# A depthwise convolution stage with tokens in eight phases and block-Toeplitz weights, on eight Trainium2 cores

## The chip, the cores and the metric

The kernel runs on all 8 cores of one Trainium2 chip. Each core takes half of one of the four sequences, that is 2048 tokens plus a halo, and no core talks to another. The metric is device time in microseconds (us) of the slowest core. A program on all eight cores has a second, slower state in some executions: the cores of one die, or of both, show a lower granted TensorE clock, and the time is some per cent longer. A ratio is the mean time of one kernel's fast runs over the mean of the other's of the same rounds, so it is not quite the ratio of the medians quoted beside it. The brackets behind a ratio are its 95% interval.

## The reference, cut to what matters

The function is one encoder block. Only the convolution branch and the pooling branch matter here; the gates, the output projections and the SwiGLU part are unchanged in what they compute.

```python
def conformer_conv(a_val, a_gate, w_dw, b_dw, ln_g, ln_b, w_conv_out):
    a = a_val * jax.nn.sigmoid(a_gate)                       # (B, T, 1024)
    pad = CONV_KERNEL // 2                                   # CONV_KERNEL = 31
    a = lax.conv_general_dilated(
        a, w_dw[:, None, :].astype(a.dtype), window_strides=(1,), padding=[(pad, pad)],
        dimension_numbers=("NWC", "WIO", "NWC"), feature_group_count=a.shape[-1]) + b_dw
    a = jax.nn.silu(layer_norm(a, ln_g, ln_b))               # over the channels
    return a @ w_conv_out

# multi_scale_pool: for four channel groups, a centred window mean (windows 2, 4, 8, 16)
# over the tokens minus the token itself, then linear maps.      [...]
```

## The kernel before

Activations lie with 128 channels on the partitions and tokens along the free axis. The 1024 channels are 8 blocks of 128. One block of the convolution stage is: project value and gate (80 matmuls of 416 columns, in five pieces), multiply value by sigmoid(gate) into `aT`, store that to `ad` in device memory, and load it back four times, shifted by 0 to 3 tokens, as an im2col operand `rep` with 32 channels by 4 shifts on the partitions. The convolution of the block before runs between two projections. It multiplies `rep` with weights that GpSimd builds from a mask. Four matmuls of 32 output channels run side by side in four column tiles of the PE array.

```python
def vg(c):                                   # value and gate of block c
    for p in range(NPC):                     # 5 pieces of 416 tokens
        ...                                  # 8 + 8 matmuls into two PSUM banks
        act(s_, bg_[:, 0:PW], AF.Sigmoid)
        tt(DVE, aT[c % 2][:, sl], bv[:, 0:PW], s_, ALU.mult)
        if p == 2:
            a_out(c, 0, 3 * PW)              # SyncE stores the first three pieces
        pump(2)                              # two queued pooling-window operations on VectorE
    a_out(c, 3 * PW, EXT)

def conv(c):
    pump_until(win_done, c)
    for b in range(NB):                      # 4 tiles of 512 tokens
        ps = nb()
        for q in range(8):
            for j in range(4):               # 4 column tiles of 32 channels
                ...                          # matmul 128x32 weights, 512 columns
        act(d_sb[c][b][:], ps[:], AF.Identity, bias=pcc(PC_BDW, c))
        ...                                  # squares; sums on VectorE for the LayerNorm
        pump(1)
    if c + 2 < KC:
        build_cw(c + 2)                      # GpSimd multiplies mask and weights

for c in range(1, KC):
    vg(c)
    conv(c - 1)
    im2col(c)                                # SyncE: wait for the stores, 8 loads
```

Three dots mark cuts, here and in the other listings. DMA work is issued in order by the engine named in the call: SyncE (`SP`) for activations, GpSimd (`POOL`) for weights.

## Time and profile before

| | before |
|---|---|
| time, median of 3 | 1033.84 us (1032.79 to 1034.22) |
| span of the profiled core (core 7) | 1039.7 us |
| TensorE busy | 1005.6 us, 97% |
| one block of the convolution stage | 21.2 us = 14.17 + 7.02 |

The profile's page of the kernel before: busy time, then the span in 40 slices with the busy share in tenths (and for PEclk the granted clock in tenths), then DMA packets, then the chain of work that ended last by engine and by line.

```profile
span 1039.7 us, 15674 instructions; the slowest of 8 cores (1026.0 to 1039.7 us)
...
PE 1005.6 (97%) x5696; PEld 489.7 (47%) x5696; DVE 450.1 (43%) x693; ACT 307.6 (30%) x500; POOL 158.0 (15%) x182
...
PE   3899999999999999999999999999999999999997
...
PEclk9999999999989999999999999999999999999999
...
DMA packets 34251, 99.90 MB, mean 96 GB/s; under 512 B 3968, under 2 KB 7168, under 8 KB 31616
...
PE 91%; DMA 4%; DVE 2%; ACT 1%; issue 1%; SPq 0%; POOL 0%; DVEq 0%; ACTq 0%; POOLq 0%
PE ps L353 86%; PE ps L628 5%; DMA rep_186<-ad 2%; DMA xb_178<-xp 1%; DVE uT L374 1%; DMA ad<-aT_183 1%; DVE sqx L367 1%; DMA wslot_68<-w_pool_out 0%; ACT sqx L364 0%; ACT ps L364 0%; DVE h2b_259 L374 0%; ACT L364 0%; SPq L190 0%; ACT zt_197 L364 0%; ACT zt_203 L364 0%
```

The chain is TensorE almost alone: between the first two slices and the last there is none below 9 tenths. The chain in order of time (start, duration, what) shows the block's period. L353 is the projection, L628 the convolution.

```profile
142.44 7.02 PE ps L628 x128
149.46 14.17 PE ps L353 x80
163.63 7.02 PE ps L628 x128
170.66 14.17 PE ps L353 x80
```

The busy time by stretch (columns: stretch, length, then busy us and instructions of PE, PEld, DVE, ACT, POOL, then clock, DMA share and GB/s) shows that VectorE is nearly as full as TensorE in this stage.

```profile
156.00:182.00 26.00, 26.00 (x237) 13.73 (x236) 24.85 (x37) 8.70 (x15) 6.48 (x3) 1.00 0.67 144
182.00:208.00 26.00, 26.00 (x265) 13.52 (x266) 25.03 (x36) 8.20 (x15) 7.62 (x5) 1.00 0.69 149
```

So in the middle of the convolution stage, from about 144 to 222 us, three resources are near their limits at once: TensorE at 100%, VectorE at 24.85 and 25.03 of 26 us, and the DMA engines at two thirds. (Before and after that VectorE has 11 to 19 busy us in 26.) TensorE's gaps over 0.4 us from 92 to 309 us add up to 4.1 us.

### The profile page before, as it was taken

To read this page: it belongs to the slowest core of one execution; us is meant where nothing else is said; L and a number is where in the kernel's file an instruction comes from. 1 tells how busy PE (TensorE), PEld (TensorE's weight loads), DVE (VectorE), ACT (ScalarE), POOL (GpSimd) and SP (SyncE) were. 2 spreads that over 40 slices of the span, in tenths; PEclk is the share of its full clock that TensorE was granted. 3 is DMA by queue.
4 is the path that set the end of the run, shared out by engine and by line. 5 is a ranking of instruction groups with operands and counts; after the bars stand their busy time and mean duration, and the time that the engine had idled before them with its cause. 6 is when DMAs were issued, how large, how long until landed. Compare 5 with 4: busy or idle time off the path is not lost.

```text
span 1039.7 us, 15674 instructions; the slowest of 8 cores (1026.0 to 1039.7 us)
## 1 busy us (share of the span) xinstructions
PE 1005.6 (97%) x5696; PEld 489.7 (47%) x5696; DVE 450.1 (43%) x693; ACT 307.6 (30%) x500; POOL 158.0 (15%) x182
## 2 busy tenths in 40 slices
PE   3899999999999999999999999999999999999997
PEld 1645555555434444444444444444444444444486
DVE  4542789974278532233546521212121221342454
ACT  2643333343487612211144311111111111121121
POOL 2143122221420000000167001111000000000000
PEclk9999999999989999999999999999999999999999
DMA  9705876667254111111887446655222202403112
GB/s 215 212 1 94 177 165 145 149 155 157 50 88 65 31 31 31 31 21 21 209 317 154 100 79 96 95 85 83 35 35 34 32 1 92 151 39 124 81 82 82
DMA packets 34251, 99.90 MB, mean 96 GB/s; under 512 B 3968, under 2 KB 7168, under 8 KB 31616
## 3 DMA queue, kind: packets, MB, share of 16 engines
q0 software_dynamic: 17888, 45.10, 24.6%
q1 hardware_dynamic: 16288, 53.81, 17.8%
q8 instruction: 47, 0.77, 0.3%
q14 instruction: 28, 0.23, 0.1%
HBM read 111.93 MB, written 21.04 MB: 128 GB/s over the span
## 4 chain that ended last, share of the span: by engine, by line
PE 91%; DMA 4%; DVE 2%; ACT 1%; issue 1%; SPq 0%; POOL 0%; DVEq 0%; ACTq 0%; POOLq 0%
PE ps L353 86%; PE ps L628 5%; DMA rep_186<-ad 2%; DMA xb_178<-xp 1%; DVE uT L374 1%; DMA ad<-aT_183 1%; DVE sqx L367 1%; DMA wslot_68<-w_pool_out 0%; ACT sqx L364 0%; ACT ps L364 0%; DVE h2b_259 L374 0%; ACT L364 0%; SPq L190 0%; ACT zt_197 L364 0%; ACT zt_203 L364 0%
## 5 line engine op out<-in xcount | busy, mean ns | idle before, releaser
L353 PE MATMUL ps<-mT,weff 128*128 128x512 bf16 x256 | 60.7, 386 | 0.0
L353 PE MATMUL ps<-uT,wslot_60 128*128 128x512 bf16 (+6 forms) x224 | 51.8, 356 | 5.9 <-DVE uT L374 5.3
L353 PE MATMUL ps<-uT,wslot_65 128*128 128x512 bf16 (+6 forms) x216 | 47.1, 366 | 0.0
L364 ACT ACTIVATE sgf_225<-ps 128x512 f32<-128x512 f32 x30 | 17.9, 597 | 81.3 <-PE ps L353 77.6
L364 ACT ACTIVATE sgf_226<-ps 128x512 f32<-128x512 f32 x29 | 17.3, 597 | 82.1 <-PE ps L353 82.1
L364 ACT ACTIVATE sgf_227<-ps 128x512 f32<-128x512 f32 x29 | 17.3, 597 | 79.8 <-PE ps L353 79.8
L353 PE MATMUL ps<-uT,wslot_61 128*128 128x416 bf16 (+6 forms) x192 | 40.6, 358 | 0.0
L353 PEld LDWEIGHTS ps<-mT,weff 128*128 128x128 bf16 x256 | 25.4, 99 | 31.4 <-issue 4.6
L353 PE MATMUL ps<-uT,wslot_62 128*128 128x416 bf16 (+6 forms) x192 | 39.5, 352 | 0.0
L353 PE MATMUL ps<-uT,wslot_64 128*128 128x416 bf16 (+6 forms) x192 | 38.8, 346 | 0.0
L353 PE MATMUL ps<-vT,wslot_64 128*128 128x512 bf16 x160 | 38.2, 382 | 0.0
L353 PE MATMUL ps<-vT,wslot_62 128*128 128x512 bf16 x160 | 38.2, 382 | 0.0
L353 PE MATMUL ps<-vT,wslot_67 128*128 128x512 bf16 x160 | 38.1, 380 | 0.0
L353 PE MATMUL ps<-vT,wslot_66 128*128 128x512 bf16 x160 | 38.0, 380 | 0.0
L353 PEld LDWEIGHTS ps<-uT,wslot_60 128*128 128x128 bf16 x224 | 21.8, 98 | 34.2 <-issue 16.1
L353 PE MATMUL ps<-vT,wslot_63 128*128 128x512 bf16 x160 | 37.8, 379 | 0.0
L353 PE MATMUL ps<-vT,wslot_68 128*128 128x512 bf16 x160 | 37.8, 379 | 0.0
L353 PE MATMUL ps<-vT,wslot_65 128*128 128x512 bf16 x160 | 37.8, 379 | 0.0
L353 PE MATMUL ps<-vT,wslot_61 128*128 128x512 bf16 x160 | 37.8, 379 | 0.0
L353 PEld LDWEIGHTS ps<-uT,wslot_65 128*128 128x128 bf16 x216 | 21.3, 100 | 22.5 <-issue 3.2
L353 PE MATMUL ps<-uT,wslot_68 128*128 128x416 bf16 (+1 forms) x144 | 30.9, 357 | 0.0
L353 PE MATMUL ps<-vT,wslot_60 128*128 128x512 bf16 x128 | 30.2, 379 | 0.0
(1681 smaller groups left out, 1973.7 us busy)
## 6 DMA issues: line engine op xcount, KB each, us to landing
rep_185<-ad SPq DMA_DIRECT2D x32, 263.0 KB, 6.2
rep_186<-ad SPq DMA_DIRECT2D x32, 263.0 KB, 7.5
h2b_259<-h1d SPq DMA_DIRECT2D x2, 2048.0 KB, 9.1
h1b_216<-xr POOLq DMA_DIRECT2D x1, 2048.0 KB, 14.1
h1b_217<-xr SPq DMA_DIRECT2D x1, 2048.0 KB, 15.6
h1b_218<-xr SPq DMA_DIRECT2D x1, 2048.0 KB, 19.2
h1b_219<-xr SPq DMA_DIRECT2D x1, 2048.0 KB, 24.3
h1d<-h1b_216 SPq DMA_DIRECT2D x1, 2048.0 KB, 15.3
```

Of the source, the lines that this page charges most:

```text
L353: S.op(PE, lambda e: e.matmul(out, lhsT=lhsT, rhs=rhs, start=start, stop=stop), [lhsT, rhs], [out], signal=stop if signal is None else signal)
L364: S.op(ACT, lambda e: e.activation(out=out, in_=in_, func=func, scale=scale, **kw), reads, [out])
L367: S.op(eng, lambda e: e.tensor_tensor(out=out, in0=a, in1=b, op=op), [a, b], [out])
L374: S.op(eng, lambda e: e.scalar_tensor_tensor(out=out, in0=a, scalar=s, in1=b, op0=op0, op1=op1), [a, b] + ([] if isinstance(s, float) else ...
L628: S.op(PE, lambda e, o=o, lt=lt, r_=r_, q=q, j=j: e.matmul(o, lhsT=lt, rhs=r_, start=(q == 0), stop=(q == 7), tile_position=(0, 32 * j)), ...
```

## The change

The intent is to do the convolution with fewer, fuller matmuls. Tokens are kept in phase order throughout: token 8n + h goes to phase h, column n. In the convolution the 128 partitions then hold 16 channels by 8 phases. The 31 taps of one channel become a banded (Toeplitz) matrix from 8 input phases to 8 output phases, for five column shifts. A group of 16 channels is five 128x128 matmuls of 256 columns, and a block is 8 groups, so 40 matmuls instead of 128. The price is:

- The layout on the partitions changes twice. `a` goes to device memory piece by piece and comes back permuted as `aP`; the results go out as `dst` and come back permuted as `dall`. All of this is issued by SyncE, in order. A block's results are four tiles of two groups each, and there are three buffers `dst`. So ScalarE can evict the fourth tile (copy it out of PSUM, where the matmuls write) only when the store of the first tile, called store 0 below, has landed.
- The Toeplitz weights `cw` come from device memory, 2.6 MB of float32 a block, cast to 1.3 MB of bfloat16 by the DMA that GpSimd issues.
- The pooling windows cannot run over one row of tokens any more; each step splits in two at the phase boundary.

The core of the diff, with cuts marked:

```diff
-    aT = [at(f"aT{i}", [128, EXT], BF16, z + i * EXT * 2) for i in range(2)]
-    rep = [...]
+    cw = [at(f"cw{i}", [128, NG, NSH, 128], BF16, o) for i, o in enumerate((oW + 4096, oZ))]
+    aT = [at(f"aT{i}", [128, PW], BF16, z + i * PW * 2) for i in range(NAT)]      # NAT = 6
+    aP = [at(f"aP{i}", [128, NG, PN], BF16, z + i * NG * PN * 2) for i in range(2)]
+    dst = [at(f"dst{i}", [128, 2, ON], F32, z + i * 2048) for i in range(3)]      # three buffers
 [...]
+    def load_cw(c):
+        S.dma(POOL, cw_sem[c % 2], cw[c % 2][:].rearrange("p g s m -> p (g s m)"), cw_d.ap()[c])
 [... in vg(c), per piece p:]
-            tt(DVE, aT[c % 2][:, sl], bv[:, 0:PW], s_, ALU.mult)
-            pump(2)
+            tt(DVE, aT[r][:], bv[:, 0:PW], s_, ALU.mult)
+            S.dma(SP, ad_sem[r], a_d.ap()[c].rearrange("g (q h) n -> (g q) (h n)", h=NPH)[:, sl], aT[r][:])
+            pump(4)
 [... at its end:]
+        for p in range(NPC):
+            S.wait_prod(SP, ad_sem[(NPC * c + p) % NAT])
+        S.dma(SP, rep_sem[c % 2], aP[c % 2][:], a_d.ap()[c].rearrange("g p n -> p g n"))
 [... conv(c):]
+        for t in range(4):
+            ps = nb()
+            for i in range(2):
+                for s_ in range(NSH):
+                    mm(ps[:, i * ON:(i + 1) * ON], cw[c % 2][:, 2 * t + i, s_, :],
+                       aP[c % 2][:, 2 * t + i, s_:s_ + ON], s_ == 0, s_ == NSH - 1, ...)
+            r = (4 * c + t) % 3
+            [... ScalarE evicts the tile to dst[r] and its squares to dsq; VectorE adds both to sums]
+            S.dma(SP, dw_sem[r], dc_d.ap()[c][2 * t:2 * t + 2].rearrange("g p n -> p g n"), dst[r][:])
             pump(1)
+        for r in range(3):
+            S.wait_prod(SP, dw_sem[r])
+        S.dma(SP, dr_sem[c], dall[c][:], dc_d.ap()[c].rearrange("g (q h) n -> (g q) (h n)", h=NPH))
         if c + 2 < KC:
-            build_cw(c + 2)
+            load_cw(c + 2)
```

## The prediction

> **What bounds it now.** TensorE is busy 97% of the span and makes 91% of the chain that ended last, at a granted clock of 0.99. The change touches the convolution stage, about 92 to 290 us. By the timeline, one channel block there lasts 21.2 us: 80 value/gate matmuls of 416 columns (14.17 us) and 128 convolution matmuls of 128x32 weights (7.02 us; four column tiles run together). VectorE is just as full: 24.9 and 25.0 of 26 us busy from 156 to 208 us (busy time by stretch). TensorE hardly waits in this stage: 0.6 us before convolution 0 and 1.7 us before the last one, both for the im2col loads. DMA is busy 67 to 78%.
>
> **What the change removes.** A block's convolution becomes 40 matmuls of 256 columns. The output projection's 256-column bf16 matmuls start 0.109 us apart in this trace, so 4.36 us in place of 7.02: 2.66 us a block, 21 us in all. The four-fold im2col loads (2.1 MB a block, 145 ns a 2104-byte packet) go, and so does GpSimd's weight building, beside which one VectorE add took 2.1 us in place of 0.87.
>
> **What it adds**, a block:
> - DMA: ready Toeplitz weights, 1.3 MB after the cast (128 packets; the 5632-byte cast packets took 436 ns, so about 6.3 us of all 16 engines); convolution results out in 1024-byte packets (46 ns: 2.9 us) and back (8192-byte, 309 ns: 2.5 us); a permuted load in 520-byte packets (estimate 2 us); `a` out, 1.5 us; projection weights as before, 2.8 us. The sum, an estimate, is 18 us in a period that ought to be 18.6.
> - VectorE: the pooling windows go from 84 adds and subtractions to 164 smaller ones. Dependent ones start n/0.96 ns + 0.26 us apart, so I estimate 89 us in place of 81. With 4 issued a piece, a block needs 19 to 22 us. VectorE, not TensorE, then sets the pace, which alone cancels most of the gain.
> - A new wait. SyncE issues in order: last `a` piece, wait for it to land, permuted load, then the four result stores. The stores use three buffers, so ScalarE's eviction of tile 3 waits until store 0 lands, and holds a PSUM bank, the sigmoids and VectorE's sums behind it. Unloaded: 2.3 (an `a` store takes 2.2) + 0.5 + 5 + 1.5 for the eviction, some 9 us after the last `a`; then 12.6 us of VectorE work: 21 us. The Toeplitz load, issued when the convolution ends, falls into just that window. The Trainium skill, "DMA: Bandwidth & Descriptors", section "Issuing engines are not separate DMA queues", says that all queues' DMAs run on the same 16 engines and interleave; here an `a` store beside weight loads took 5.6 us, one without 2.2. I add 2 to 5 us: 23 to 26 us a block.
>
> **On the critical path.** Six blocks at +1 to +5 us, less the last convolution's 2.7 and the im2col waits: -10 to +40 us. All else is unchanged.
>
> **Predicted: 1047 us**, 8 in 10 from 1018 to 1080. Faster by over 2%: 0.14; within 2%: 0.44; slower by over 2%: 0.42.
>
> **Right if** the convolution matmuls start 0.11 us apart, but TensorE has a gap of several us a block, after the convolution, ended by ScalarE's eviction, itself waiting for the store of `dst`; VectorE is idle in its sums at that time; DMA is busy over 80%; and after the stage nothing changes. **Wrong if** store 0 lands within 4 us of its eviction (then VectorE alone limits, about 1025), if VectorE's small operations cost less (about 1015), or if DMA falls behind altogether (over 1080).

## The result, and the profile after

The changed kernel takes **1099.2 us** (median of 4 runs, 1095.56 to 1102.62) against 1034.03 for the kernel before in the same rounds. The ratio is **1.0632 [1.0596, 1.0668]**: slower by 6.3%, above the range of the prediction (1018 to 1080).

The profile's page of the changed kernel, the same lines as before:

```profile
span 1101.0 us, 14690 instructions; the slowest of 8 cores (1080.9 to 1101.0 us)
...
PE 988.2 (90%) x5008; PEld 499.6 (45%) x5008; DVE 454.5 (41%) x779; ACT 314.5 (29%) x566; POOL 131.0 (12%) x182
...
PE   3899675666686899999999999999999999999997
...
PEclk9999897888898999999999999999999999999998
...
DMA packets 47672, 114.02 MB, mean 104 GB/s; under 512 B 4080, under 2 KB 27760, under 8 KB 42992
...
PE 77%; DMA 14%; ACT 3%; DVE 3%; issue 2%; SPq 0%; POOL 0%; ACTq 0%; DVEq 0%; POOLq 0%
PE ps L367 77%; DMA dcd<-dst_168 3%; DMA dcd<-dst_169 2%; DMA dcd<-dst_170 2%; DMA ad<-aT_162 1%; DMA ad<-aT_164 1%; DMA xb_153<-xp 1%; DVE uT L388 1%; DMA wslot_65<-w_pool_out 1%; DMA aP_166<-ad 1%; DVE sqx L381 1%; ACT dsq_172 L378 1%; DMA ad<-aT_163 0%; SPq L197 0%; DMA ad<-aT_161 0%
```

Read the ledger first. TensorE is busy 17.4 us less (1005.6 to 988.2); the change was meant to save 21. But the span less TensorE's busy time grew from 34.1 to 112.8 us, by 78.7. The sum, +61.3, is the difference of the two spans. (The profiled run of the kernel before took 1041.25 us, 7 above its median; between the medians the difference is 65.2.) The slices say where: 5 to 8 tenths from the 5th to the 14th slice, the convolution stage, and the same 9s as before elsewhere. The chain now has 14% DMA in it, and the stores `dcd<-dst` lead that part.

The period of a block, from one block's last piece of `a` to the next block's, was 21.2 us before. Now the six blocks that follow one another take 28.5, 37.9, 31.6, 31.1, 31.7 and 27.9 us. They sum to 188.7, against 128.0 before: +60.7, nearly all of the spans' difference. (Outside these blocks the savings and losses cancel.)

One such block in the changed kernel, the chain in order of time:

```profile
250.97 0.60 DVE aT_165 L381
...
251.63 2.02 DMA ad<-aT_165
...
253.82 0.37 SPq L197
...
254.29 13.25 DMA dcd<-dst_169
...
268.46 0.36 ACT dst_169 L378
268.82 0.37 ACT dsq_172 L378
...
269.33 11.25 PE ps L367 x58
```

And the timeline around it (start, duration, engine, line, operation, out<-in; in brackets the idle time before and what ended it):

```profile
248.44 4.55 PE L367 MATMUL ps<-aP_166,cw_158 128*128 128x256 bf16 x40
...
253.54 0.53 POOL L197 DMA_DIRECT2D cw_158<-cwt  x1 [3.82 <-PE ps L367]
253.82 0.37 SPq L197 DMA_DIRECT2D aP_167<-ad  x1
...
254.29 0.53 SPq L197 DMA_DIRECT2D dcd<-dst_169  x1
254.91 7.23 SPq L197 DMA_DIRECT2D dcd<-dst_170  x1
...
267.62 0.47 ACT L378 ACTIVATE dst_169<-ps,pc_s 128x256 f32<-128x256 f32 x1 [11.65 <-DMA dcd<-dst_169]
...
268.93 0.69 DVE L381 TENSOR_TENSOR acc_s<-acc_s,dst_169 128x512 f32<-128x512 f32 x1 [9.92 <-ACT dst_169 L378]
269.33 2.93 PE L367 MATMUL ps<-uT,wslot_63 128*128 128x416 bf16 x8 [10.71 <-ACT dsq_172 L378]
```

The convolution itself is as fast as hoped: 40 matmuls in 4.55 us, where 4.36 were predicted and 7.02 were needed before. Then comes the wait. The last piece of `a` is ready at 251.57; its store lands at 253.65; SyncE issues the permuted load at 253.82 and store 0 at 254.29. But at 253.54, just ahead of both, GpSimd had issued the Toeplitz load. Store 0 lands 13.25 us after its issue. Only then may ScalarE evict the convolution's fourth tile, into the buffer that store 0 leaves. The eviction holds up VectorE (idle 9.92 us) and TensorE (10.71 us). SyncE's second store is itself stuck in its issue for 7.23 us.

The trace's DMA packets of this core, counted in steps of 2 us, show what happened in those 13 us:

```
us      Toeplitz  permuted   a store  result store  share of the
        10240 B   520 B      832 B    1024 B        16 engines
252         0        0        128         0           0.25
254        13        0          0         0           0.56
256        23       22          0         0           0.74
258        32       32          0         0           1.11
260        30       30          0         0           0.87
262        30      196          0         0           0.93
264         0      744          0       292           1.08
266         0        0          0       476           0.70
```

The two loads take turns, one packet each. A Toeplitz packet has 10240 bytes and takes about 0.8 us of an engine; a permuted packet has 520 bytes and takes 0.028. So the permuted load gets 15 packets a microsecond beside the Toeplitz load and over 370 after it. It waits for nearly the whole Toeplitz load, and the stores, in the same queue, wait behind it. The Trainium skill, "DMA: Bandwidth & Descriptors", section "Queues, rings and completion order", says that an engine takes turns between the queues that have work, a packet at a time; the counts of 23 to 22, 32 to 32 and 30 to 30 agree with that. The page counts 9 to 17 descriptors to a packet as typical; what takes turns here are single runs of 10240 and 520 bytes.

The page's list of DMA issues (out<-in, engine, count, KB each, median us from issue to landing):

```profile
cw_158<-cwt POOLq DMA_DIRECT2D x4, 1280.0 KB, 11.8
cw_159<-cwt POOLq DMA_DIRECT2D x4, 1280.0 KB, 13.0
...
dcd<-dst_169 SPq DMA_DIRECT2D x11, 256.0 KB, 6.7
```

Two smaller things. The eight matmuls after the gap took 2.93 us where 1.57 is usual, and the eight after those 1.79; the granted clock was 0.50 from 262.3 to 272.4 us. That fits the Trainium skill, "TensorE: Matmul & The Clock Gate", section "What's actually happening", which says that TensorE drops to half its clock after an idle window of about 3.4 us; the prediction had no term for it, some 1.6 us a gap here. And the busy time by stretch shows VectorE, full before, now busy 6.6 and 13.4 of 26 us (at most 20.2 in the stretches from 208 to 312 us), so it does not set the pace here:

```profile
156.00:182.00 26.00, 8.06 (x39) 4.01 (x38) 6.62 (x14) 2.90 (x7) 0.00 (x0) 0.67 0.75 172
182.00:208.00 26.00, 15.53 (x104) 9.86 (x101) 13.42 (x31) 7.16 (x19) 1.58 (x3) 0.86 0.73 167
```

What TensorE waited for from 90 to 380 us (total us, times, longest) is this. The first line is the wait just described, at six convolutions; the other two are the first convolution's permuted load and the LayerNorm sums:

```profile
PE ps L367 <- ACT dsq_172 L378: 61.9, 6, 17.9
PE ps L367 <- DMA aP_166<-ad: 8.6, 1, 8.6
PE ps L367 <- DVE acc_s L381: 8.4, 1, 8.4
```

### The profile page after: what moved, and what is told of

Its sections match the earlier page's. It is cut to its first block, busy times and chain, and to the rows that moved or that the text cites. A ratio compares the mean times of both kernels' runs of the same rounds, so it can differ in the third digit from the quotient of the medians.

```text
span 1101.0 us, 14690 instructions; the slowest of 8 cores (1080.9 to 1101.0 us)
## 1 busy us (share of the span) xinstructions
PE 988.2 (90%) x5008; PEld 499.6 (45%) x5008; DVE 454.5 (41%) x779; ACT 314.5 (29%) x566; POOL 131.0 (12%) x182
## 3 DMA queue, kind: packets, MB, share of 16 engines
q0 software_dynamic: 19040, 55.58, 28.8%
## 4 chain that ended last, share of the span: by engine, by line
PE 77%; DMA 14%; ACT 3%; DVE 3%; issue 2%; SPq 0%; POOL 0%; ACTq 0%; DVEq 0%; POOLq 0%
PE ps L367 77%; DMA dcd<-dst_168 3%; DMA dcd<-dst_169 2%; DMA dcd<-dst_170 2%; DMA ad<-aT_162 1%; DMA ad<-aT_164 1%; DMA xb_153<-xp 1%; DVE uT L388 1%; DMA wslot_65<-w_pool_out 1%; DMA aP_166<-ad 1%; DVE sqx L381 1%; ACT dsq_172 L378 1%; DMA ad<-aT_163 0%; SPq L197 0%; DMA ad<-aT_161 0%
## 5 line engine op out<-in xcount | busy, mean ns | idle before, releaser
L367 PE MATMUL ps<-uT,wslot_65 128*128 128x416 bf16 (+5 forms) x128 | 26.1, 354 | 28.8 <-ACT dsq_172 L378 28.8
L367 PE MATMUL ps<-uT,wslot_61 128*128 128x416 bf16 (+6 forms) x192 | 41.4, 364 | 10.2 <-ACT dsq_172 L378 10.2
L367 PE MATMUL ps<-uT,wslot_63 128*128 128x416 bf16 (+6 forms) x192 | 40.0, 354 | 10.7 <-ACT dsq_172 L378 10.7
L367 PEld LDWEIGHTS ps<-uT,wslot_59 128*128 128x128 bf16 x224 | 22.3, 100 | 44.1 <-issue 26.4
L367 PE MATMUL ps<-uT,wslot_60 128*128 128x416 bf16 (+6 forms) x192 | 41.9, 366 | 0.0
L367 PE MATMUL ps<-vT,wslot_66 128*128 128x512 bf16 x160 | 38.0, 379 | 0.0
L367 PE MATMUL ps<-vT,wslot_65 128*128 128x512 bf16 x160 | 37.8, 379 | 0.0
L367 PE MATMUL ps<-vT,wslot_62 128*128 128x512 bf16 x160 | 37.8, 379 | 0.0
L367 PE MATMUL ps<-vT,wslot_60 128*128 128x512 bf16 x160 | 37.8, 379 | 0.0
L367 PE MATMUL ps<-vT,wslot_67 128*128 128x512 bf16 x160 | 37.8, 379 | 0.0
L367 PE MATMUL ps<-vT,wslot_63 128*128 128x512 bf16 x160 | 37.8, 379 | 0.0
L367 PE MATMUL ps<-vT,wslot_61 128*128 128x512 bf16 x160 | 37.8, 379 | 0.0
L367 PE MATMUL ps<-vT,wslot_64 128*128 128x512 bf16 x160 | 37.8, 379 | 0.0
L367 PEld LDWEIGHTS ps<-uT,wslot_61 128*128 128x128 bf16 x192 | 19.7, 104 | 28.1 <-issue 12.2
L367 PEld LDWEIGHTS ps<-uT,wslot_63 128*128 128x128 bf16 x192 | 18.8, 99 | 28.0 <-issue 12.4
```

The source lines that it names most:

```text
L367: S.op(PE, lambda e: e.matmul(out, lhsT=lhsT, rhs=rhs, start=start, stop=stop), [lhsT, rhs], [out], signal=stop if signal is None else signal)
```

## The experiments

The theory after reading the profile: the fourth tile waits for store 0, and the Toeplitz load makes that wait long, because it meets SyncE's chain (last `a` store, permuted load, stores) on the same 16 DMA engines. The rivals: DMA work as such (the bytes do not fit the block, wherever they are put), and VectorE's greater number of window operations. Sixteen kernels ran. They are compared with the kernel before in the same rounds. Its median over its fast runs lay between 1032 and 1035 us in all rounds, so a difference of a few us between runs of different rounds says little. Diffs are against the changed kernel unless said.

For four of the kernels the next table splits the wait of each convolution in two, read from the profiled core's instructions: from the last piece of `a` to the issue of the permuted load (an `a` store's landing), and from there to the fourth tile's eviction (the load's turn and store 0's landing). The first convolution is left out; its wait is another one, told above.

| us, convolutions 1 to 6 of each | last `a` ready to permuted load issued | permuted load issued to fourth tile evicted |
|---|---|---|
| predicted, unloaded | 2.3 | 5.5 |
| changed kernel | 18.7, 4.6, 3.9, 2.3, 1.9, 5.5 | 6.2, 12.9, 12.2, 13.8, 13.5, 8.1 |
| Toeplitz matrices loaded for two blocks only | 5.1, 5.3, 4.0, 1.9, 1.9, 5.6 | 6.9, 7.1, 5.0, 5.1, 5.1, 5.7 |
| Toeplitz load a piece later | 9.9, 9.9, 8.2, 5.9, 6.3, 9.9 | 6.3, 5.4, 5.4, 5.4, 5.7, 5.1 |
| Toeplitz load after the stores | 10.2, 9.9, 7.7, 5.4, 4.6, 7.9 | 5.4, 5.6, 5.6, 5.8, 4.9, 5.6 |

### A fourth buffer for the results

```diff
+    dst.append(at("dst3", [128, 2, ON], F32, oW + 14336))
-            r = (4 * c + t) % 3
+            r = (4 * c + t) % 4
```

(and a fourth semaphore to go with it).

> The changed kernel with a fourth staging buffer for the convolution results, so that the eviction of a block's tile 3 no longer waits for the store of tile 0. Theory W (the wait for the store is what costs): the six gaps of TensorE after the convolution (10.2 to 17.9 us each, 71 us with the one at the LayerNorm sums left out) go almost wholly, and a block falls from 31 us to what VectorE needs, 20 to 21.5 us; the time becomes about 1037 us (1028 to 1048). Rival B (the 16 DMA engines can't carry a block's 18 to 21 us of packets any faster): the gaps move to the waits for the permuted load in front of the convolution, and the time stays over 1060. Rival V (VectorE's split windows set the pace): under 10 us of change.

Measured: 1063.2 us, ratio 1.0313 [1.0269, 1.0357]. The wait for the eviction is gone, which shows that the three buffers made it. But 40 us of a new wait came in its place, and the total is the rival's. TensorE's waits in this run, and two lines of SyncE's timeline:

```profile
PE ps L368 <- DMA aP<-ad: 40.0, 7, 9.4
PE ps L368 <- DVE acc_s L382: 2.4, 1, 2.4
...
228.39 0.33 SPq L197 DMA_DIRECT2D dall<-dcd  x1
228.82 3.75 SPq L197 DMA_DIRECT2D ad<-aT  x5
```

So some 35 us of the loss (1099.2 less 1063.2, in other rounds) was the buffer. The rest of it moved one step up SyncE's chain, to the permuted load itself. That the total is the rival's does not make the rival's cause shown. In this run SyncE waits for the result stores to land before it issues the reload of the results at 228.39 us, and the five `a` stores of the next block, the last of them ready since 220.60, are issued only behind it. So the order of issue makes part of the new wait, whatever the bytes are.

### The Toeplitz matrices loaded once

Blocks 0 and 1 load theirs; the others use these again. The result is wrong (relative error 0.355).

```diff
-        if c + 2 < KC:
-            load_cw(c + 2)
```

> The changed kernel with the Toeplitz weights loaded for blocks 0 and 1 only; blocks 2 to 7 use them again, so the result is wrong on purpose. Three staging buffers as before. Theory W with the collision (the large Toeplitz packets, taken turn by turn with the permuted load's small ones, hold up the store by 8 us): the store lands 5 to 6 us after its issue in place of 12 to 13, the gap falls from 10.5 to 2 to 3 us, the block to about 22 us; 1045 us (1035 to 1058). If the wait came from SyncE's order alone (waits for the last a store), the gap would fall by under 3 us: over 1075.

Measured: 1057.81 us (median of four, one of them slow), ratio of the fast runs 1.0238 [1.0219, 1.0256]. With the same three buffers, taking away the six loads takes away 41 us. In the table the second column falls from 12 to 14 us to 5 to 7, near the predicted 5.5. The remaining waits are TensorE's 19.3 us for the eviction, the first convolution's 8.7 and the LayerNorm's 8.7. Its six blocks still take 28.8, 25.9, 26.5, 24.0, 22.6 and 19.8 us, so without any Toeplitz load beside them most are over the 21 us of the prediction's unloaded case. The run has fewer bytes as well as no collision, so it does not yet tell these two apart.

### Stores on ScalarE's queue

```diff
-            S.dma(SP, dw_sem[r], dc_d.ap()[c][...], dst[r][:])
+            S.dma(ACT, dw_sem[r], dc_d.ap()[c][...], dst[r][:])
```

> The changed kernel with the four result stores of a block issued by ScalarE on its own queue, each right after its eviction, with three staging buffers. Theory W: store 0 is under way before the Toeplitz load is issued and doesn't stand behind the permuted load, so it lands 2.5 to 4 us after its eviction and tile 3 hardly waits; 1038 us (1028 to 1050), much as with a fourth buffer, for the same bytes and packets. Rival B: over 1060.

Measured: 1060.63 us, ratio 1.0269 [1.0252, 1.0285]. The wait for the eviction falls to 10.7 us in three places, since stores no longer stand behind the permuted load; the permuted load is waited for instead, 23.9 us. This is much the same gain as the fourth buffer's, and it stops at the same place. The gain is as the theory has it; the 22 us that are missing to its number speak for the rival, or for the order of issue as in the run before.

### The Toeplitz load a piece later

```diff
+            if p == 1 and 2 <= c:            # in vg(c), second piece of the next block
+                S.wait_prod(POOL, DVE)
+                load_cw(c)
-        if c + 2 < KC:
-            load_cw(c + 2)
```

> The changed kernel with each Toeplitz load (blocks 2 to 7) held back until VectorE has gated the second piece of the next block, so that it no longer meets the permuted load and the stores; bytes, packets and the three buffers are the same. Theory W with the collision: as with the weights loaded once, gap 2 to 3 us, block 22 us, 1047 us (1036 to 1060). Rival B (total bytes): no change, over 1085.

Measured: 1081.19 us, ratio 1.0474 [1.0451, 1.0497]: a miss by 34 us. The table shows why. The permuted load and the stores are now quick (5.1 to 6.3 us), but the Toeplitz load runs at the time of the `a` stores, and the last of these takes 5.9 to 9.9 us. TensorE still waits 37.6 us for the eviction. The collision was not avoided; it met another link of the same chain.

### The late load, cut into small packets

The load of the experiment before, in eight parts, so that its packets have 1280 bytes.

```diff
-        S.dma(POOL, cw_sem[c % 2], cw[c % 2][:].rearrange("p g s m -> p (g s m)"), cw_d.ap()[c])
+        tot = cw_sem[c % 2].count + 16 * NG
+        for g in range(NG):
+            S.dma(POOL, cw_sem[c % 2], cw[c % 2][:, g].rearrange("p s m -> p (s m)"),
+                  cw_d.ap()[c][:, g * NSH * 128:(g + 1) * NSH * 128], val=tot)
```

> As e6_late (Toeplitz load held back, three buffers, same bytes), but each Toeplitz load cut into eight of one group, so that its packets are 1280 bytes in place of 10240. In e6 the load met the last a store instead of the permuted load, and the two took turns packet by packet. Theory T (turns are taken by packets, whatever their size): a small packet waits behind 0.11 us in place of 0.8 us, the last a store lands some 3 us after its issue in place of 6 to 7, and the chain a store, permuted load, store 0 gets 4 to 6 us shorter in each of six blocks: 1056 us (1046 to 1068) against 1081 for e6. Rival (the engines share by bytes, or are simply full): 1076 or more.

Measured: 1081.61 us, ratio 1.0463 [1.0416, 1.051]: no gain. The `a` packets did pass faster: 129 of them beside 212 Toeplitz packets from 234 to 236 us, against 45 beside 36 in the run before from 238 to 240 us. But the last `a` store still took 6.6 to 7.9 us where 3 were expected (5.7 to 9.7 in the run before). The test is not clean, though. A 1280-byte packet took a median of 116 ns where an eighth of a whole one would take 100 (799 ns), and the six loads together took 63 us of all engines' time in place of 47. Whether small packets would help at equal work is left open.

### All waits removed

Fourth buffer, stores on ScalarE's queue, and the Toeplitz matrices loaded once. Wrong (relative error 0.355).

> Fourth buffer, stores on ScalarE's queue, and the Toeplitz weights loaded for blocks 0 and 1 only (wrong result on purpose): the wait for the store and a third of the DMA work are both gone, VectorE's work is as in the changed kernel. If VectorE's split windows set the pace of what is left (19.5 to 21.5 us a block, my estimate): 1031 us (1026 to 1040), with VectorE busy over 90% of a block and no gap of TensorE over 2 us in the middle blocks. If VectorE does not matter: TensorE's pace of 18.6 us a block, 1018 us or less. If something else waits that I have not seen: over 1042.

Measured: 1034.44 us, ratio 1.0011 [0.9987, 1.0034]. TensorE's gaps in the stage are 8.0 us before the first convolution and otherwise at most 2.1, with 3.3 at the LayerNorm sums. The block's periods after the first are 18.6, 19.6, 20.6, 21.7 and 15.7 us. Without a wait for DMA the pace is still not TensorE's 18.6, and the reason is VectorE's time by stretch (the third number group):

```profile
156.00:182.00 26.00, 26.00 (x165) 15.91 (x164) 25.06 (x54) 11.76 (x28) 1.05 (x2) 1.00 0.74 191
182.00:208.00 26.00, 26.00 (x176) 17.02 (x175) 24.65 (x50) 11.61 (x28) 2.14 (x4) 1.00 0.81 211
208.00:234.00 26.00, 24.14 (x155) 14.65 (x154) 24.64 (x48) 10.86 (x26) 1.07 (x2) 1.00 0.60 175
```

This bounds what VectorE takes: with the DMA waits out of the way, but for the first convolution's 8.0 us and one of 2.1, the changed kernel is level with the kernel before.

### The same, with the windows spread evenly

The run before, with three window operations a piece in place of four from block 4 on; with four all along, the last block had few left.

```diff
-            pump(4)
+            pump(4 if c < 4 else 3)
```

> As e8_waitless (fourth buffer, stores on ScalarE's queue, Toeplitz weights loaded for blocks 0 and 1 only, so the result is wrong on purpose) with one thing more: three window pieces a projection piece in place of four from block 4 on. Blocks 4 to 6 of e8 took 19.6 to 21.7 us with VectorE busy 24.6 of 26 us. If that was VectorE's windows: 18.6 to 19.2 us a block, 1027 us (1021 to 1032), 6 to 8 us under e8. If not: no change from 1034.

Measured: 1028.25 us, ratio 0.9948 [0.9924, 0.9972], as expected (also wrong, 0.355). The periods are 18.4, 17.7, 18.7, 18.9 and 18.1 us. So VectorE's uneven pace was worth 6 us, and about TensorE's 18.6 us a block is reached when these DMA waits are out of the way.

### Legal combinations in float32

Legal here means that the result is right. The first puts together: four buffers, the stores' own queue, even windows, the Toeplitz load held to the first piece and cut, and block 0's Toeplitz load issued one stage earlier.

> A correct kernel with all cures that keep the bytes: fourth buffer, stores on ScalarE's queue, window pieces spread more evenly (4 a piece for blocks 0 to 3, then 3), the Toeplitz load cut into 1280-byte packets and held back to the first piece of the next block, the first Toeplitz load issued before the last pooling tiles (the 8.6 us gap before convolution 0 should go). Estimate: the DMA work of 18 to 20 us a block is then the limit: 1034 us (1022 to 1050).

Measured: 1055.12 us, ratio 1.0207 [1.0185, 1.023]; a miss by 21 us. The first convolution's gap is gone, the blocks without a gap take 18.4 to 19.7 us, but three gaps of 17.0, 5.5 and 10.4 us wait for the permuted load. The second has the whole Toeplitz load at its original place:

> Correct kernel, f32 all through: fourth buffer, stores on ScalarE's queue, even window pieces, first Toeplitz load early; Toeplitz loads whole (10240-byte packets) and issued where the change issues them. Against e9 only the cutting into 1280-byte packets and the holding back are undone; the cut loads took 63 us of engine time for six in e7, the whole ones 47 in the changed kernel. If DMA work is the limit: 8 to 20 us under e9's 1055, 1040 us (1028 to 1050).

Measured: 1055.0 us, ratio 1.0217 [1.0175, 1.0259]; again a miss, by 15 us. There is no gap before the first convolution, where the changed kernel has 8.6 us: with the Toeplitz load of block 0 out of the way its permuted load is issued at 113.0 us in place of 120.9. TensorE still waits 23.4 us for permuted loads:

```profile
PE ps L368 <- DMA aP<-ad: 23.4, 2, 11.8
PE ps L368 <- DVE sb L382: 6.3, 1, 6.3
```

Both places of the Toeplitz load give 1055. Whether the place hardly matters once the buffers are right is not shown by that, since the first of these runs also cut the load, which took more of the engines' time above.

### The same with results in bfloat16

The results go out and come back in bfloat16: 4.2 MB less each way a core. Each is paired with one of the two runs above.

```diff
-    dc_d = nc.dram_tensor("dcd", [KC, NG, 128, ON], F32, kind="Internal")
+    dc_d = nc.dram_tensor("dcd", [KC, NG, 128, ON], BF16, kind="Internal")
```

(and `dst` and `dall` likewise). The outputs are right.

> As e9, but the convolution results make their way out to memory and back in bf16, which takes 2 to 2.5 us of DMA work from a block (512-byte and 1024-byte packets in place of 1024 and 8192). If DMA work is what limits e9: 10 to 20 us faster than e9, 1022 us (1012 to 1036). If it isn't: as e9 within 5 us. The result is a little less exact.

Measured: 1042.98 us, ratio 1.0085 [1.0032, 1.0138]; 12 us less than in float32, within the 10 to 20 that were expected; the total is over the expected range, since the float32 run had missed its own.

> As e12, with the convolution results going out and back in bf16: 2 to 2.5 us of DMA work less in a block. Every wait I know of then fits into TensorE's 18.6 us: 1020 us (1010 to 1034), if so faster than the kernel before by 0 to 2%. If it stays over 1034, DMA work is still the limit.

Measured: 1031.8 us, ratio 1.0001 [0.9965, 1.0038], 23 us less than in float32. Waits for the permuted load fall from 23.4 to 8.2 us. So in this state fewer bytes do help, as the rival has it for what is left once the buffer wait is cured. What remains comes from order as well: SyncE issued a reload of results at 180.82 us, and five waiting `a` stores only at 181.45, behind it.

### Bfloat16, Toeplitz load held to the first piece

The run just told, with the load of the next block held to the first piece, and one projection tile moved ahead of the LayerNorm sums.

> As e11, with the Toeplitz load held back to the first piece of the next block (uncut), so that the permuted load goes first, and a projection tile moved in front of the first LayerNorm sums, where TensorE waited 3 us. 1017 us (1008 to 1034); the holding back may cost or save some us against e11, since the load then meets the a stores.

Measured: 1042.91 us, ratio 1.0066 [1.0002, 1.013] (one run slow): worse, not better, with gaps of 11.2, 9.6 and 4.7 us. The held load meets the `a` stores again, as in the float32 run with the late load.

### The reload of results deferred

SyncE reloads a block's results only after the next block's permuted load, so that it never stands ahead of `a` stores. LayerNorm order as in the last run. The Toeplitz load is at its original place.

```diff
-        for r in range(4):
-            S.wait_prod(SP, dw_sem[r])
-        S.dma(SP, dr_sem[c], dall[c][:], ...)
+        def reload():
+            [the same three lines]
+        later.append(reload)          # run after the next permuted load
```

In float32:

> As e12 (f32 all through, 1055 us), but the reload of a block's results is issued one block later, after the next block's permuted load, so that SyncE no longer waits for the stores in front of the next a pieces; and one projection tile goes in front of the first LayerNorm sums (2 to 3 us). Bytes and packets are those of e12. If the order of the waits on SyncE is what is left: the waits for the permuted load (11.7, 6.3 and 11.8 us in e12) shrink to 2 us or less each, 1022 us (1014 to 1034). If the engines' total DMA work is what is left: 1045 us or more.

Measured: 1044.87 us, ratio 1.0102 [1.0064, 1.014], 10 us better than without the deferral (of other rounds; some of it is the LayerNorm order, whose wait had been 4.0 us), and at the rival's number. In two of its four runs, the profiled one among them, a pair of cores ran at a clock of 0.96 and set the time. The profiled core's gaps add up to only 12.3 us (41.2 without the deferral), but that flatters the run: its granted clock was 0.81 from 197 to 358 us, and a TensorE at that clock leaves its transfers more time. The six cores of the same execution without that stretch have gaps of 18 to 26 us, against 25 to 41 on the cores without the deferral. The two runs without such a pair took 1040.05 and 1042.58 us. So a run with such a pair is some 7 us longer, and one without it still some 19 us over the expected 1022; how much of that is DMA work stays open.

In bfloat16:

> As e11 (results out and back in bf16, 1032 us) with the same two moves. Each middle block of e11 waits 1.8 to 3.5 us for its permuted load because SyncE holds the a pieces back until the stores have landed. If that wait goes: TensorE's own 18.6 us a block, 1017 us (1010 to 1025), faster than the kernel before by 1 to 2%. If total DMA work is the limit: 1030 us.

Measured: ratio 0.9955 [0.9888, 1.0021]. Its runs: 1023.26, 1024.2, 1026.0, one of 1038.1 with two cores at a clock of 0.966, and two slow (1037.39, 1152.57). Not resolved by this interval.

### The Toeplitz load after the stores, nothing else changed

The runs so far had altered the bytes, or had moved the load onto another link. This one leaves the changed kernel's three buffers and all its bytes, and only issues the Toeplitz load when the block's stores have landed. (The record below says the first three stores; the fourth shares its semaphore with the first, so the edit waits for all four.)

```diff
         if c + 2 < KC:
+            for r in range(3):
+                S.wait_prod(POOL, dw_sem[r])
             load_cw(c + 2)
```

> The changed kernel with its three buffers and the same bytes; the only edit is that GpSimd issues the next block's Toeplitz load after the first three stores of the block have landed, so that the permuted load and the stores have the DMA engines without it. Theory (the collision with the Toeplitz load is the term I sized too small): the time from the last a piece to the eviction of the fourth tile, 17.4 us in the changed kernel, falls to about 10 us; a block falls from 31 to 22-25 us; total 1050 to 1065, close to the run that loads the Toeplitz matrices once (1058). Rival (the work of the bytes alone sets it, whenever they move): 1080 or more, with gaps before the fourth tile of 7 us or more, or gaps of the same sum that wait for the Toeplitz load.

Measured: 1082.7 us, ratio 1.0495 [1.0473, 1.0516]. The total is the rival's, and from the last `a` piece to the fourth tile it takes 9.5 to 15.6 us (the two columns of the table together) where 10 were expected. But the split says something sharper. The chain in order of time in one of its blocks:

```profile
179.23 9.62 DMA ad<-aT
...
189.02 0.37 SPq L197
...
189.49 5.09 DMA dcd<-dst
```

Store 0 lands 5.09 us after its issue, where the changed kernel's took 13.25; in the table the second column is 4.9 to 5.8 us in all six blocks, which is the 5.5 that the prediction had for the unloaded case. So at equal bytes the collision with the Toeplitz load is what had added 8 us there. But the load now falls on the next block's `a` stores: this one took 9.62 us where the other took 2.02. The packet counts show it: from 180 to 182 us 32 Toeplitz packets and 32 `a` packets, and then, since GpSimd issues the projection weights behind the Toeplitz load, 155 weight packets and 156 `a` packets from 184 to 186. TensorE's gaps fall from 84.1 to 52.7 us, no further. With the late load above, which met the same stores, this suggests that SyncE's chain, from the first `a` store to the last result store, fills so much of the block that a load of 12 to 16 us finds no place beside it.

### The best version: permuted load first

The deferred bfloat16 run, with one more wait, so that the Toeplitz load starts when the permuted load has landed. The stores have their own queue and a fourth buffer here, so they can bear the delay.

```diff
         if c + 2 < KC:
+            S.wait_prod(POOL, rep_sem[(c + 1) % 2])
             load_cw(c + 2)
```

> The run with four buffers, stores on their own queue, even windows, bfloat16 results and deferred reload, plus: GpSimd issues the Toeplitz load only after the permuted load of the next block has landed. If what is left there is the collision of these two loads: waits for the permuted load vanish, 1018 (1012 to 1028). If it is the sum of the DMA work or VectorE's pace: 1023 to 1034 as without the edit.

Measured: 1023.13 us, five runs (1021.47 to 1024.07), ratio 0.9911 [0.9896, 0.9927]. It is 0.9% under the kernel before, clear of 1 by its interval. The number lies at the border of the two expectations, and the waits did not vanish, as the first had it: one permuted load late in the stage was still waited for.

```profile
PE ps L367 <- DMA aP<-ad: 11.7, 3, 9.5
```

Against the deferred run without this wait the difference is not measured in the same rounds; its undisturbed runs of 1023 to 1026 are close to this, and its profiled core waited only 4.1 us for permuted loads. So it is not shown that the added wait helped.

## Why the prediction was right or wrong

**What bounds it before: right.** TensorE, with VectorE and DMA close behind. The runs bear this out: with the DMA waits taken away VectorE set the pace, and with VectorE's work spread as well TensorE about did.

**What the change removes: right.** Predicted 2.66 us a block; measured 7.02 - 4.55 = 2.47.

**The DMA work added: right in size.** The Toeplitz packets took a median of 799 ns, 6.4 us a block of all engines (predicted 6.3; by the sum of all packets, the slowed ones with them, 47 us for six loads, 7.9 each); the packets of 520, 1024 and 8192 bytes took 28, 46 and 309 ns as assumed.

**VectorE: right, but hidden.** "VectorE, not TensorE, then sets the pace" was true only without DMA waits (1034 and 1028 us, with four and with evenly spread window operations). Its rule for small operations, n/0.96 ns + 0.26 us, is a fit to the trace of the kernel before: dependent ones of 512, 683 and 1024 columns started 0.796, 0.965 and 1.329 us apart, where it gives 0.793, 0.971 and 1.327. In the changed kernel VectorE waits with the rest.

**The wait through three buffers: right in mechanism.** The chain is link for link the predicted one. In the block at 250 us the `a` store took 2.0 us, the issue of the permuted load 0.5 and the eviction at the end 1.6 (267.62 to 269.20), where 2.3, 0.5 and 1.5 were predicted. Without the Toeplitz load on it the last link is 5 to 6 us, as predicted.

**The step that failed: "I add 2 to 5 us: 23 to 26 us a block".** This is the term for the Toeplitz load's collision. It measured 8 us in the link of the permuted load and store 0 (13.25 in place of 5.09 at equal bytes), in four of the six convolutions of the table; in the first of the six the collision hit the `a` stores instead, by 16 us (18.7 in place of 2.3). The last of the six has no Toeplitz load beside it: its `a` store took 5.2 us beside 2048-byte weight packets, and why its second link took 8.1 us is open. The mistake was to scale an `a` store's delay beside weight loads, 2.2 to 5.6 us, to this case. Those were weight packets of 2048 bytes beside `a` packets of 1664 and 2496. Here each 520-byte packet waits for a 10240-byte one, so the permuted load hardly moves until the Toeplitz load is through, and the collision costs most of the length of that load (8.2 of the 11.4 us from its issue to its landing), not a fair share of it. The blocks then took 31.1 to 31.7 us where 23 to 26 were predicted, one took 37.9, and the six together +60.7 us, where "six blocks at +1 to +5 us" gave +6 to +30. A smaller part is the base: "unloaded", 21 us, was too low as well, since most blocks took 22.6 to 26.5 us with the six loads gone.

**What the sum lacked altogether.** First, the first convolution: its permuted load was late by 8.6 us of TensorE time, since the two first Toeplitz loads ran beside its `a` stores (one took 12.8 us from 107.96). With block 0's load issued a stage earlier there was no such gap. Second, the slow clock after each gap, about 1.6 us. Third, 8.4 us at the LayerNorm sums after the last convolution, which has nothing behind it to cover the wait.

**"DMA is busy over 80%": wrong.** It was 0.75 and 0.73 in the stretches shown and 0.61 to 0.77 from 130 to 312 us. While each step of the chain waits for the one before, the engines stand idle at times (a share of 0.25 from 252 to 254 us). The prediction's condition for going over 1080, "if DMA falls behind altogether", therefore does not describe what happened: 1099 came with DMA a quarter idle or more.

**What the rival kept.** With the buffer wait cured, 1055 us in float32 against 1031.8 in bfloat16 shows that fewer bytes help next. And delaying the load alone, at equal bytes, gained only some 16 us. What stays open is how the last 10 us of the float32 version (1044.87 us, against 1034 before) divide between DMA work, order of issue and packet sizes, and whether smaller packets at equal work would end the starving.

## What to carry to other kernels

When a kernel is near the limit of three resources, a saving on one is worth what the other two leave of it: here TensorE was busy 17 us less and idle 79 us more, until the DMA chain was shortened. When a large load with big packets shares the DMA engines with a small-packet transfer that something waits for, count the delay as nearly the whole length of the large load, not as a share. Before you move a load out of the way, list the links of the waiting chain in time: a load that is longer than every hole in the chain only meets another link, and then buffers, fewer bytes or a separate issuing queue are what helped here.

## What the Trainium skill lacked or had wrong

- "DMA: Bandwidth & Descriptors", section "Queues, rings and completion order": it has the turns by packets, but not what unequal packets do. A load of 520-byte packets moved at 15 packets a microsecond beside 10240-byte packets, and at over 370 after them. Its "≈9-17 descriptors typical" to a packet do not fit here: the turns went by single runs, 32 of 10240 bytes to 32 of 520 in 2 us on 16 engines.
- The same page, section "Issuing engines are not separate DMA queues", says that the sequencer's time to initiate a DMA "is usually small relative to the DMA itself". Here one issue on SyncE took 7.23 us, while the earlier transfers of its queue were held up, and the engine's later issues stood behind it.
- The same page gives the cast during DMA as a feature, under "SWDGE vs HWDGE vs iDMA", but no rate. Here a packet of 10240 bytes after the cast (20480 before it) took a median of 799 ns, where a plain packet of the same 10240 bytes in the kernel before (input activations in float32) took a median of 397 ns: 26 bytes a nanosecond in both, an estimate from these two, if the bytes before the cast are counted. Cut to 1280 bytes a packet took 116 ns, a sixth more per byte.
- "TensorE: Matmul & The Clock Gate", section "What's actually happening", is borne out: after a gap of 10.7 us, with the granted clock at 0.50, eight matmuls took 2.93 us in place of 1.57.
